# The second MLP product of a diffusion layer as seven block products per pass, with weight sums made by accumulating transfers

## The chip, the core and the metric

The kernel runs on one core of one Trainium2 chip. The metric is device time in microseconds (us), the median of the runs shown. All arithmetic is 32-bit. A large product is made as three TensorE passes: each operand is split into a rounded part ("hi", ScalarE) and the rest ("lo", VectorE), and hi·hi, hi·lo and lo·hi are summed in PSUM. Engines are called as in the profile: PE (TensorE), DVE (VectorE), ACT (ScalarE), POOL (GpSimd) and SP (SyncE, which only issues transfers).

## The reference, cut to what matters

One layer over 512 latent tokens and 256 context tokens of width 1024: modulation vectors from a condition, a modulated norm, an input projection, windowed attention beside a gated delta rule, an output projection with a residual, and an MLP of hidden width 4096 with a second residual. The last step is the one that is changed:

```
def mlp(s, shift, scale_m):
    hm = rms_norm(s, g_norm2) * (1.0 + scale_m) + shift
    return jnp.square(jax.nn.relu(hm @ w_mlp1)) @ w_mlp2
x_new = x_new + gt2 * mlp(x_new, sh2, sc2)
```

## The kernel before, in words

**Front (0 to about 45 us).** SP issues the loads in the order of a list: the latent tokens `xT` (four of 512 KB), the condition, the parameters, then sixteen 512 KB pieces of the modulation weights (`in_wada`, line 148), with three early weight tiles and the context tokens between them. While they land, PE runs 30 matmuls on a tile of ones (line 230, `NONES`); each takes two rows of the trace. `norm_x` squares the tokens on ACT (line 402), adds on DVE (405) and sums over partitions on PE (406); ACT makes the reciprocal root (line 185 is the helper for ACT). For each of eight k-tiles, `ada` multiplies the condition by its weights (249), `columns` turns the row into columns (272) and DVE makes scale and shift (281, 282); `features` modulates (339 on DVE, 340 on ACT, 341 on DVE) and `early_x` feeds the early tiles (331, 333, 335). More ones-matmuls (276 `NWAIT`, 434 `WARM`) stand between these.

**MLP (about 520 us to the end).** The hidden width is worked through in four passes of 1024 (`hf` 0 to 3). Pass 0 makes its part of the first product tile by tile. Passes 1 to 3 make it by class `Pair`: two hidden tiles at a time, as seven block products of half tiles (Strassen's method in Winograd's form; line 1612 issues all its matmuls, 336 of 128x256 in a pass). The operand sums of the weights are made on DVE, in SBUF. `Pair.second` squares the result, splits it and appends it to `act_`.

In each pass the second product follows, channel-major: for each of eight tiles of output channels one load of 512 KB (`w2`, line 290), a split (ACT line 295, DVE line 300), 24 matmuls of 128x512 (8 hidden tiles by 3; lines 331, 333, 335), and one DVE operation (line 1739) that scales the PSUM tile by `gt2` and adds it to the residual `xn_` in SBUF. After pass 3 each `xn_` tile is stored (line 1742), and the host transposes the result.

**Order.** Within an engine the order is set before the run: `Lists` plays the program through with costs and picks the next instruction of each engine by rank; the table `SHIFTS` moves ranks by hand. At run time each engine works through its own list in order and waits on semaphores, so an instruction that waits holds up all that stand behind it on its engine. Buffers of the arena (`alloc`, `free`) come free in program order. POOL issues the transfers that add to their destination (`accum_op`, so far line 298: 16 weight tiles of the input projection get their lo part that way), SP the plain ones.

Of the kernel before, what the change touches and what calls it, by code (L numbers as in the profile page):

```python
# [10 lines left out]
F32 = mybir.dt.float32  # L11
# [18 lines left out]
NONES, NWAIT = 30, 8  # L30
# [8 lines left out]
WARM = (0, 3, 3, 3, 2, 0, 0, 0)  # L39
NROWS = 2  # L40
ND1 = 3
NGD = 5
P = 128
D = 1024
# [73 lines left out]
def tile_layer(ctx: ExitStack, tc: tile.TileContext, I: dict, out: bass.AP, dbg=None):  # L118
# [72 lines left out]

    cc = cload("cc", [P, KT, 2])
# [65 lines left out]
    xs_, cs_ = alloc(8 * SEQ), alloc(8 * CTX)  # L258
    for k2 in range(KT // 2):
        nc.sync.dma_start(out=xs_[:, k2 * 1024:(k2 + 1) * 1024], in_=I["xT"][k2])  # L260
# [86 lines left out]
    for k4 in range(KT // 4):  # L347
        nc.sync.dma_start(out=cs_[:, k4 * 1024:(k4 + 1) * 1024], in_=I["ctxT"][k4])
# [47 lines left out]
    def norm_x():  # L396
        ss = bank()
        for i in range(4):
            b = alloc(1024)
            src = xs_[:, i * 1024:(i + 1) * 1024]  # L400
            n = 512 if i == 3 else 1024
            A.activation(b[:, :n], src[:, :n], AF.Square)
            if i == 3:
                V.tensor_tensor(b[:, n:], src[:, n:], src[:, n:], op=ALU.mult)
            V.tensor_tensor(b[:, :512], b[:, :512], b[:, 512:], op=ALU.add)
            PE.matmul(ss.ap, ones, b[:, :512], start=(i == 0), stop=(i == 3))
            b.free()
        act(rx, ss.ap, AF.Ln, bias=epsc, scale=1.0 / D)
        ss.free()
        return act(rx, rx, AF.Exp, scale=-0.5)  # L410
# [5 lines left out]
    load_early()  # L416
# [5 lines left out]
    features(1)  # L422
    columns(2, ada(2))
    load_early()
# [1142 lines left out]
    class Pair:  # L1567
# [67 lines left out]
        def second(self):  # L1635

            w, z = bank(), bank()
            o = self.o
            self.prod(w[:, :256], "12", "21")
            V.tensor_tensor(o[:, :256], self.u[:, :256], w[:, :256], op=ALU.add)  # L1640
            w.free()
            self.u.free()
            self.prod(z[:, :256], "22", "T4")
            self.prod(z[:, 256:], "S4", "22")
            V.tensor_tensor(o[:, 256:768], o[:, 256:768], z.ap, op=ALU.add)
            z.free()
            A.activation(o.ap, o.ap, AF.Relu)
            A.activation(o.ap, o.ap, AF.Square)
            hi, lo = alloc(1024), alloc(1024)
            split(o.ap, hi.ap, lo.ap)  # L1650
            o.free()
            act_.extend([hi, lo])
            for i in range(2):
                xs.append((r32(hi[:, i * 512:i * 512 + 512]), r32(lo[:, i * 512:i * 512 + 512])))

    def combos():
# [25 lines left out]
        xs7 = {"11": mh[0][:4], "12": mh[0][4:], "22": mh[1][4:]}  # L1682
# [4 lines left out]

    FT = 8
    pairs = [[Pair(hf * FT + f) for f in range(0, FT, 2)] if hf else [] for hf in range(4)]
    for hf in range(4):  # L1690
        act_, xs = [], []
        for f in range(0 if hf else FT):
# [7 lines left out]
            r, hl = alloc(1024), alloc(1024)  # L1700
            A.activation(r[:, :512], acc.ap, AF.Relu)
            acc.free()
            V.tensor_tensor(r[:, 512:], r[:, :512], r[:, :512], op=ALU.mult)
            split(r[:, 512:], hl[:, :512], hl[:, 512:])
            for b in bufs + [r]:
                b.free()
            act_.append(hl)
            xs.append((r32(hl[:, :512]), r32(hl[:, 512:])))
            next(late)
        if hf == 0:  # L1710
            xs7 = combos()
            for _ in late:
                pass
            scr_[0].free()
            for b in MH[0]:
                b.part(1024, 1024).free()
        w2 = lambda ct: wload(I["wm2"][ct * 4 + hf])
# [9 lines left out]
        ws = [w2(0), w2(1)]  # L1727
        if hf:
            ps_[-1].second()
        accs = [bank(), bank()]  # L1730
        ks = list(range(FT))
        for cols in (ks[:FT - 2], ks[FT - 2:]):
            for acc, w in zip(accs, ws):
                mm3(acc.ap, w, [xs[k] for k in cols], start=(cols[0] == 0), stop=(cols[-1] == FT - 1), ks=cols)
        for ct in range(8):
            if ct > 1:
                accs.append(bank())
                mm3(accs[ct].ap, w2(ct), xs)
            V.scalar_tensor_tensor(xn_[ct], accs[ct].ap, modT[:, 3, ct:ct + 1], xn_[ct], op0=ALU.mult, op1=ALU.add)  # L1739
            accs[ct].free()  # L1740
            if hf == 3:
                nc.sync.dma_start(out=out[ct], in_=xn_[ct])
            if hf < 3 and ct in (3, 5):
                (pairs[hf + 1][0].load1 if ct == 3 else pairs[hf + 1][0].load2)()
        for b in act_:
            b.free()
        if hf < 3:
            pairs[hf + 1][1].load1()
# [140 lines left out]
class Lists:  # L1889

    ENGINES = ("PE", "DVE", "Activation", "Pool", "SP")

# [46 lines left out]
    def run(self, rank):  # L1939
# [4 lines left out]
        free, links = [0., 0., 0., 0., 750.], [0., 0., 0., 0., 3200.]  # L1944
# [3 lines left out]
        rows, done = [None, None], [0., 0.]  # L1948
# [22 lines left out]
        for _ in range(n):  # L1971
# [16 lines left out]
            if self.dma[k]:  # L1988
                if e == 4:
                    if len(flight) >= 8:  # L1990
                        t = max(t, flight[-8])
                    links[e] = end = max(t + (2400 if self.bytes[k] > 100000 else 1600), links[e]) + self.bytes[k] / 422
                    flight.append(end)
                    free[e] = t + 400
                else:
                    links[e] = end = max(t + 2400, links[e]) + self.bytes[k] / 159
                    free[e] = t + 900
            else:
                own, lag = self.cost[k]
                if e == 0:  # L2000
                    words, had = words + self.words[k], words
                    block = int(words / 256 + .63)
                    if block > int(had / 256 + .63):
                        asked[block] = max(t + 1100, links[4] - 500) + 1250
                    t = max(t, asked.get(int(had / 256 - .54), 0))
# [5 lines left out]
                if e in (1, 2):  # L2011
                    if self.rows[k] != rows[e - 1]:
                        t, rows[e - 1] = max(t, done[e - 1] + 28), self.rows[k]
                    done[e - 1] = t + lag
                end = t + lag
# [74 lines left out]
def pack(i):  # L2090
# [31 lines left out]
    m2 = i["w_mlp2"][0].reshape(4, 8, P, 8, P)  # L2122
    a["wm2"] = np.ascontiguousarray(m2.transpose(3, 0, 2, 1, 4).reshape(32, P, KT, P))
# [41 lines left out]
```

## Time and profile before, and how to read it

| what | value |
|---|---|
| median of 3 runs | 866.34 us (865.48 to 866.76) |
| the profiled execution | 865.59 us, of which 863.5 us are its span |
| granted TensorE clock, mean | 0.997 |
| PE, DVE, ACT, POOL busy | 98%, 75%, 58%, 3% of the span |
| read from memory, written | 103.61 MB, 2.10 MB |

A busy PE in this table is the union of matmul durations, which overlap: a 128x512 matmul is shown with 0.39 us, while the next one starts 0.23 us later. What a matmul costs is therefore read from the distance of two starts. The same holds, less strongly, for DVE. In the views, a row of the windows gives the stretch, its length, and for each engine the busy time with the number of instructions in brackets; then the granted clock, the mean busy share of the 16 DMA engines, and GB/s. A row of the timeline gives start, duration, engine, line, operation, and tiles with their shapes.

### The profile page before, as it was taken

What the parts mean: (1) busy time and instruction counts of PE and PEld (TensorE: products, weight loads), DVE (VectorE), ACT (ScalarE), POOL (GpSimd) and SP (SyncE); (2) the same over time, 40 slices, a digit from 0 to 9 for tenths busy, and PEclk for the clock granted to TensorE, in tenths of its full rate; (3) what the DMA queues carried; (4) which work ended last, traced back from release to release, by engine and by line L of the source; (5) the groups of instructions that cost most, each with busy time, mean ns of one, the idle gap of its engine ahead of it and who ended that gap; (6) DMA issues with size and microseconds to landing.
All of it is one profiled execution on the core that took longest, in us unless ns stands there. A gap on an engine that the chain in (4) does not pass through costs nothing.

```text
span 863.5 us, 17980 instructions
## 1 busy us (share of the span) xinstructions
PE 849.9 (98%) x7544; PEld 715.2 (83%) x7544; DVE 643.9 (75%) x1113; ACT 497.4 (58%) x882; POOL 26.0 (3%) x42
## 2 busy tenths in 40 slices
PE   9999999999999999899999999999999999999998
PEld 6688778877778777687787899888998899889986
DVE  3865899987779997778758879983875388549541
ACT  5569775487669895577754445651553256326510
POOL 0000011010000002000000000000000000000000
PEclk9999999999999999999999999999999999999999
DMA  9924266542211237633116845733413331343031
GB/s 356 364 75 99 61 149 137 121 98 51 37 38 37 72 93 252 212 124 101 40 52 229 284 139 162 247 119 98 146 50 97 111 135 49 98 145 100 2 121 49
DMA packets 31985, 106.86 MB, mean 124 GB/s; under 512 B 4000, under 2 KB 4512, under 8 KB 31904
## 3 DMA queue, kind: packets, MB, share of 16 engines
q1 hardware_dynamic: 29600, 97.33, 33.8%
q0 software_dynamic: 2304, 8.39, 6.1%
q8 instruction: 59, 0.97, 0.4%
q14 instruction: 22, 0.18, 0.1%
HBM read 103.61 MB, written 2.10 MB: 122 GB/s over the span
## 4 chain that ended last, share of the span: by engine, by line
PE 92%; DVE 3%; ACT 2%; DMA 1%; issue 1%; SPq 0%; ACTq 0%; DVEq 0%
PE banks L331 16%; PE banks L333 16%; PE banks L335 15%; PE banks L1612 14%; PE banks L1148 13%; PE banks L1243 3%; PE banks L1194 2%; PE banks L725 2%; DMA wr<-in_wbr 1%; PE banks L230 1%; PE banks L781 1%; PE banks L714 1%; PE banks L715 1%; PE banks L894 1%; PE banks L566 1%
## 5 line engine op out<-in xcount | busy, mean ns | idle before, releaser
L331 PE MATMUL banks<-m,wh 128*128 128x512 f32 (+1 forms) x568 | 212.2, 375 | 0.5 <-ACT wh L295 0.5
L333 PE MATMUL banks<-m,wh 128*128 128x512 f32 (+1 forms) x568 | 210.6, 371 | 0.0
L335 PE MATMUL banks<-m,wl 128*128 128x512 f32 (+1 forms) x568 | 209.9, 370 | 0.0
L295 ACT ACTIVATE wh<-wr 128x1024 fp32r<-128x1024 f32 (+1 forms) x92 | 90.5, 985 | 143.8 <-PE banks L333 104.5
L331 PEld LDWEIGHTS banks<-m,wh 128*128 128x128 f32 x568 | 107.2, 189 | 18.8 <-ACT wh L295 0.9
L1612 PEld LDWEIGHTS banks<-m,m 128*128 128x128 f32 x1008 | 121.9, 192 | 1.0 <-ACT m L224 0.3
L1612 PE MATMUL banks<-m,m 128*128 128x256 f32 x1008 | 122.6, 283 | 0.0
L335 PEld LDWEIGHTS banks<-m,wl 128*128 128x128 f32 x568 | 106.9, 188 | 18.4 <-issue 0.5
L333 PEld LDWEIGHTS banks<-m,wh 128*128 128x128 f32 x568 | 107.1, 189 | 17.7 <-issue 0.5
L224 ACT ACTIVATE m<-m 128x512 fp32r<-128x512 f32 (+2 forms) x118 | 82.4, 721 | 56.8 <-PE banks L1612 9.0
L1148 PE MATMUL banks<-m,wh 128*128 128x512 f32 x320 | 105.7, 405 | 0.8 <-ACT m L185 0.8
L225 DVE TENSOR_TENSOR m<-m,m 128x512 fp32r<-128x512 f32 (+2 forms) x118 | 91.8, 802 | 17.5 <-ACT m L224 16.8
L300 DVE TENSOR_TENSOR wl<-wr,wh 128x1024 fp32r<-128x1024 f32 (+1 forms) x76 | 84.2, 1108 | 13.3 <-ACT wh L295 10.7
L1739 DVE SCALAR_TENSOR_TENSOR m<-banks,modT,m 128x512 f32<-128x512 f32 x32 | 24.0, 750 | 78.2 <-PE banks L335 78.0
L1148 PEld LDWEIGHTS banks<-m,wh 128*128 128x128 f32 x320 | 59.5, 190 | 13.7 <-ACT m L185 1.0
L1148 PE MATMUL banks<-m,wl 128*128 128x512 f32 x160 | 64.5, 403 | 0.0
L333 PE MATMUL banks<-m,m 128*128 128x256 f32 (+1 forms) x136 | 45.8, 343 | 0.2
L511 DVE SCALAR_TENSOR_TENSOR m<-m,m 128x1024 f32<-128x1024 f32 x32 | 39.0, 1220 | 9.1 <-DMA m<-in_wada 9.0
L331 PE MATMUL banks<-m,m 128*128 128x256 f32 (+1 forms) x136 | 44.8, 340 | 0.2 <-ACT m L340 0.2
L335 PE MATMUL banks<-m,m 128*128 128x512 f32 (+1 forms) x120 | 39.5, 335 | 0.0
L1243 PEld LDWEIGHTS banks<-m,m 64*64 64x64 f32 x1600 | 26.5, 134 | 11.2 <-issue 3.9
L1148 PEld LDWEIGHTS banks<-m,wl 128*128 128x128 f32 x160 | 30.3, 189 | 6.3
(263 smaller groups left out, 1311.7 us busy)
## 6 DMA issues: line engine op xcount, KB each, us to landing
m<-in_wada SPq DMA_DIRECT2D x48, 512.0 KB, 4.8
wr<-in_wm SPq DMA_DIRECT2D x40, 512.0 KB, 3.6
wr<-in_win SPq DMA_DIRECT2D x38, 512.0 KB, 3.7
m<-in_wm SPq DMA_DIRECT2D x24, 512.0 KB, 3.7
wl<-in_win POOLq DMA_DIRECT2D x16, 512.0 KB, 5.6
m<-in_xT SPq DMA_DIRECT2D x8, 512.0 KB, 5.5
wr<-in_wbr SPq DMA_DIRECT2D x16, 256.0 KB, 2.6
wr<-in_wout SPq DMA_DIRECT2D x8, 512.0 KB, 4.5
```

The lines of the kernel that those rows point to most:

```text
L224: A.activation(r32(hi), src, AF.Copy)
L225: (eng or V).tensor_tensor(r32(lo), src, hi, op=ALU.subtract)
L295: upper[0] = A.activation(r32(hi), raw, AF.Copy)
L300: V.tensor_tensor(r32(lo), raw, hi, op=ALU.subtract)
L331: PE.matmul(acc, w[0][:, k, :], xhi, start=(start and i == 0), stop=False)
L333: r = PE.matmul(acc, w[0][:, k, :], xlo, start=False, stop=(end and w[1] is None))
L335: r = PE.matmul(acc, w[1][:, k, :], xhi, start=False, stop=end)
L511: r = V.scalar_tensor_tensor(wa.ap, wa.ap, 0.5, scr_[0].ap, op0=ALU.mult, op1=ALU.mult, accum_out=modT[:, grp, j:j + 1])
L1148: PE.matmul(acc.ap, w[x][:, k, :], hx[k][y], start=(k == p == 0), stop=(k == KT - 1 and p == 2))
L1243: runs[n].append(PE.matmul(out_, w, x, start=True, stop=True).ins.name)
L1612: PE.matmul(dst, r32(self.w[w][i][:, k * P:(k + 1) * P]), xs7[x][k][j], start=(n == 0), stop=(n == 11))
L1739: V.scalar_tensor_tensor(xn_[ct], accs[ct].ap, modT[:, 3, ct:ct + 1], xn_[ct], op0=ALU.mult, op1=ALU.add)
```

## The change

**The second product** becomes seven block products per pass (class `Down`), token-major: tokens are the rows of the PSUM tile, output channels its columns. The activations of a pass (`hb`, unsplit) are halved by hidden index and by token, the weights by hidden index and by output channel. Each product has 24 matmuls of 128x512 (line 1807 to 1809 in the new file), so 168 in a pass. Its left operands are blocks or sums of blocks of `hb`, made and split on DVE and ACT (`left`). Its weight sums are not made on an engine: `pieces` loads four half blocks and lets POOL add further blocks onto them while they are loaded from memory again (line 1733, eight transfers of 512 KB in a pass); 14 half weights are split in each pass. In pass 0 ACT copies the seven PSUM results to SBUF; in passes 1 and 2 ACT copies them and POOL adds them onto those of pass 0 by SBUF-to-SBUF transfers (line 1836, seven of 512 KB in a pass). Before pass 3, `gather` sums them across products by seven more such transfers (line 1874), multiplies by `gt2` laid out as a row, `grow` (made by eight PE transposes, line 1878; DVE, line 1888), and adds the residual from memory (line 1890, eight of 256 KB). The residual got there in pass 0: `park` transposes it on PE (32 transposes of 128x128), copies and stores it. In pass 3 the last sums are made on DVE straight from PSUM (`give`, `end`; lines 1842, 1828, 1865, 1866) and stored.

**The front:** all four `xT` loads come first; the squares are halved between ACT and DVE; the context tokens are loaded later, the second early tile earlier; the ones-matmuls go from 30 to 11, from 8 to 4 and from 11 to 6, with 4 new ones inside `norm_x` (`NSUM`). The costs of `Lists` and the table `SHIFTS` (35 entries before, 68 now) are new.

```diff
-NONES, NWAIT = 30, 8
+NONES, NSUM, NWAIT = 11, 4, 4
-WARM = (0, 3, 3, 3, 2, 0, 0, 0)
+WARM = (0, 2, 2, 2, 0, 0, 0, 0)
+LAHEAD = 1
+GAT = 0, 2
...
-            n = 512 if i == 3 else 1024
-            A.activation(b[:, :n], src[:, :n], AF.Square)
-            if i == 3:
-                V.tensor_tensor(b[:, n:], src[:, n:], src[:, n:], op=ALU.mult)
+            A.activation(b[:, :512], src[:, :512], AF.Square)
+            V.tensor_tensor(b[:, 512:], src[:, 512:], src[:, 512:], op=ALU.mult)
...
-            split(o.ap, hi.ap, lo.ap)
+            A.activation(hb[:, at:at + 1024], o.ap, AF.Square)
...
+        ORDER = ("11", "A11"), ("T3", "S3"), ("T1", "S1"), ("T2", "S2"), ("21", "A12"), ("22", "S4"), ("T4", "A22")
...
+            c = [raw(0, 0, p) for p in two]
+            d = [raw(0, 1, p) for p in two]
+            for p in two:
+                add(d[p], 1, 1, p)
+            for p in two:
+                yield halves(c[p].ap)
+                add(c[p], 0, 1, p)
+            for p in two:
+                yield halves(d[p].ap)
+                add(d[p], 0, 0, p)
+            for p in two:
+                yield halves(c[p].ap)
+                c[p].free()
+            for p in two:
+                yield halves(d[p].ap)
+                add(d[p], 1, 0, p)
+            for k in range(2):
+                for p in two:
+                    yield other(1, k, p)
+            for p in two:
+                yield halves(d[p].ap)
+                d[p].free()
...
+                for p in range(2):
+                    wh, wl = self.ready.pop(0)
+                    for tt in range(2):
+                        zz, ts_ = z[:, tt * 512:tt * 512 + 512], slice(tt * P, tt * P + P)
+                        for k in range(2):
+                            kk = 2 * p + k
+                            PE.matmul(zz, hi[:, kk, ts_], wh[:, k], start=(kk == 0), stop=False)
+                            PE.matmul(zz, hi[:, kk, ts_], wl[:, k], start=False, stop=False)
+                            PE.matmul(zz, lo[:, kk, ts_], wh[:, k], start=False, stop=(kk == 3))
...
+            if self.hf == 0 or self.hf == 3 and w in ("11", "T3", "T1"):
+                accs_[w] = alloc(1024, True)
+                A.activation(accs_[w].ap, z.ap, AF.Copy)
+                return
+            if self.hf < 3:
+                t = alloc(1024)
+                A.activation(t.ap, z.ap, AF.Copy)
+                G.dma_start(out=accs_[w].ap, in_=t.ap, accum_op=ALU.add)
...
+            if w == "T2":
+                e7, t = accs_["T3"], alloc(1024)
+                V.tensor_tensor(t.ap, e1.ap, z.ap, op=ALU.add)
+                add(e7, t)
+                add(t, e5)
+                add(e5, e7)
+                self.end("21", e7)
+                self.end("22", e5, True)
+                accs_["12"] = t
+            elif w == "21":
+                add(e1, z)
+                self.end("11", e1, True)
+            elif w == "22":
+                t = accs_["12"]
+                add(t, z)
+                self.end("12", t, True)
+            else:
+                self.end("21", z, True)
...
+            for tt in range(2):
+                y, t, x = alloc(512), ends[c][:, tt * 512:tt * 512 + 512], src[:, tt * 512:tt * 512 + 512]
+                V.tensor_tensor(y.ap, x, grow[0][:, cols], op=ALU.mult)
+                V.tensor_tensor(t, t, y.ap, op=ALU.add)
+                if store:
+                    nc.sync.dma_start(out=out[2 * r + tt][:, cols], in_=t)
...
-        w2 = lambda ct: wload(I["wm2"][ct * 4 + hf])
...
-                mm3(accs[ct].ap, w2(ct), xs)
-            V.scalar_tensor_tensor(xn_[ct], accs[ct].ap, modT[:, 3, ct:ct + 1], xn_[ct], op0=ALU.mult, op1=ALU.add)
...
+        down.run()
...
-    (0, 1732, 1922, 1869), (-1, 1465, 1789, 55), (-1, 2037, 2118, -523), (-1, 61, 266, -14), (-1, 31, 44, -137),
+    (0, 2862, 3051, 164), (-1, 115, 415, -25), (-1, 7530, 7531, 754), (-1, 4659, 4764, 98), (-1, 2017, 2101, -36),
```

**How rows move: DVE at the end of the program.** Before, the last rows are the splits of weight tiles (`wl`) and the one operation per output tile, which reads its PSUM tile (`banks`):

```order
L300 TENSOR_TENSOR wl_9034<-wr_9031,wh_9033 128x1024
L1739 SCALAR_TENSOR_TENSOR m_5687<-banks,modT,m_5687 128x512
L300 TENSOR_TENSOR wl_9066<-wr_9063,wh_9065 128x1024
L1739 SCALAR_TENSOR_TENSOR m_5687<-banks,modT,m_5687 128x512
L300 TENSOR_TENSOR wl_9098<-wr_9095,wh_9097 128x1024
L1739 SCALAR_TENSOR_TENSOR m_5687<-banks,modT,m_5687 128x512 x3
```

Now the list ends with sums in SBUF (lines 1866) and multiplications by `grow` (`m_8892`, line 1865); the two rows that read `banks` here belong to product T4, the last of all:

```order
L1866 TENSOR_TENSOR m_6697<-m_6697,m_9222 128x512
L1866 TENSOR_TENSOR m_6835<-m_6835,m_9307 128x512
L1865 TENSOR_TENSOR m_9311<-m_9207,m_8892 128x512
L1865 TENSOR_TENSOR m_9343<-banks,m_8892 128x512
L1866 TENSOR_TENSOR m_6835<-m_6835,m_9311 128x512
L1866 TENSOR_TENSOR m_6874<-m_6874,m_9343 128x512
L1865 TENSOR_TENSOR m_9212<-m_9122,m_8892 128x512
L1865 TENSOR_TENSOR m_9339<-banks,m_8892 128x512
L1866 TENSOR_TENSOR m_6874<-m_6874,m_9212 128x512
L1866 TENSOR_TENSOR m_6874<-m_6874,m_9339 128x512
```

Between the first row that reads product T2 (`m_9207<-m_9082,banks`, line 1842) and the end stand 30 DVE rows, ten of 1024 columns and twenty of 512, four of them splits of weights; before, three rows of 512 stand behind the last split.

**POOL in pass 1.** Before, POOL's list ends with fills of zeros that belong to the delta rule, and holds nothing in the MLP:

```order
L298 DMA wl_2618<-in_win 128x1024
L1017 MEMSET m_3508 32x16x32 x4
L1016 MEMSET m_3504 32x16x32 x2
L1409 MEMSET m_3898 32x16x32 x4
L1016 MEMSET m_3504 32x16x32 x2
L1408 MEMSET m_3897 32x16x32 x4
```

Now it goes on with 57 rows of transfers (61 issues). In pass 1 the additions of weights from memory (`in_wm`, to `m_7251` and `m_7253`) and of results (to the seven sums) alternate, each waiting for what it adds:

```order
L1733 DMA m_7253<-in_wm 128x1024
L1836 DMA m_6570<-m_7422 128x1024
L1836 DMA m_6610<-m_7463 128x1024
L1733 DMA m_7251<-in_wm 128x1024
L1836 DMA m_6697<-m_7507 128x1024
L1733 DMA m_7253<-in_wm 128x1024
L1836 DMA m_6739<-m_7550 128x1024
```

So the third addition onto `m_7251` stands behind two additions of results that wait for products 11 and T3.

**SP at the front.** Before, condition and parameters stand between the token loads, and the first weights of the modulation follow:

```order
L260 DMA m_123<-in_xT 128x1024 x2
L148 DMA c_cc<-in_cc 128x16
L148 DMA c_prm<-in_prm 128x188
L260 DMA m_123<-in_xT 128x1024 x2
L148 DMA m_131<-in_wada 128x1024
L148 DMA m_153<-in_wada 128x1024
```

Now the four token loads are first:

```order
L198 DMA m_71<-in_xT 128x1024 x4
L152 DMA c_cc<-in_cc 128x16
L152 DMA c_prm<-in_prm 128x188
L152 DMA m_112<-in_wada 128x1024
L152 DMA m_118<-in_wada 128x1024
L313 DMA wr_124<-in_wab 128x512
```

The last token load moves ahead of two small ones; the first weight pair keeps its place in the sequence.

More of the change, by code (lines that the diff above doesn't have):

```diff
@@ L189, in act @@
         return r
+    xs_, cs_ = alloc(8 * SEQ), alloc(8 * CTX)
+    for k2 in range(KT // 2):
+        nc.sync.dma_start(out=xs_[:, k2 * 1024:(k2 + 1) * 1024], in_=I["xT"][k2])
     cc = cload("cc", [P, KT, 2])
@@ L415, in tile_layer @@
     rp1 = ada(1)
-    load_early()
     norm_x()
@@ L1726, in tile_layer @@
                 ps_[i + 2].load1()
-        ws = [w2(0), w2(1)]
+            if hf == 3 and i in GAT:
+                next(last)
+            if i == 2:
+                down = Down(hf)
+                down.left()
         if hf:
             ps_[-1].second()
[L1730 to L1737, printed above, removed]
-                mm3(accs[ct].ap, w2(ct), xs)
[L1739 to L1746, printed above, removed]
+        if hf == 3:
+            for _ in last:
+                pass
+        down.run()
         if hf < 3:
-            pairs[hf + 1][1].load1()
+            for f in down.loads:
+                f()
     return ties, gangs
```

195 lines of the change are left out of this document (161 added, 34 removed), and 21 rows, old and new, of the table SHIFTS.

## The prediction

> **What bounds the kernel now.** I read the totals first, then the busy time by stretches, then the timeline inside the stretches that change, and last the waits and the transfers.
>
> ```profile
> PE 849.9 (98%) x7544; PEld 715.2 (83%) x7544; DVE 643.9 (75%) x1113; ACT 497.4 (58%) x882; POOL 26.0 (3%) x42
> 691.00:734.00 43.00, 43.00 (x347) 42.22 (x346) 37.05 (x60) 26.43 (x36) 0.00 (x0) 1.00 0.27 91
> 734.00:776.00 42.00, 42.00 (x190) 34.76 (x190) 20.71 (x24) 11.88 (x13) 0.00 (x0) 1.00 0.37 115
> DVE m L1739 <- PE banks L335: 78.0, 24, 4.7
> PE banks L331 <- ACT wh L295: 0.5, 1, 0.5
> ```
>
> The two stretches are pass 2: seven block products for the first MLP product (691 to 734), then the second product (734 to 776). PE is busy throughout both, at clock 1.00. DVE waits 78.0 us for PE at line 1739, while PE's own longest wait for a weight split is 0.5 us. So the MLP is bound by PE, and a PE instruction taken out of it shortens the program as long as nothing else is late. DVE is the next: 57.8 of 85.0 us in this pass.
>
> How long one matmul holds PE is the distance of starts, six apart here:
>
> ```profile
> 819.84 0.39 PE L335 MATMUL banks<-m,wl 128*128 128x512 f32 x1
> 821.20 0.39 PE L335 MATMUL banks<-m,wl 128*128 128x512 f32 x1
> 173.24 0.87 PE banks L725 x8
> ```
>
> (821.20 − 819.84) / 6 = 0.2267 us for a 128x512 matmul. The third row, from the chain that ended last, gives 0.87 / 8 = 0.109 us for a 128x128 transpose.
>
> **The change part by part.**
>
> *Matmuls.* Each pass goes from 8 x 24 = 192 matmuls to 7 x 24 = 168: over four passes 96 x 0.2267 = **21.8 us less**. The residual's transposes (32) and those of the gate row (8) are new on PE: 40 x 0.109 = **4.4 us more**; they stand in PE's list between products, so nothing hides them. A pass now lasts about 85.0 − 5.4 = 79.6 us.
>
> *DVE and ACT in a pass.*
>
> ```profile
> L300 DVE TENSOR_TENSOR wl<-wr,wh 128x1024 fp32r<-128x1024 f32 x60 | 73.2, 1220 | 6.4 <-ACT wh L295 4.1
> L224 ACT ACTIVATE m<-m 128x1024 fp32r<-128x1024 f32 x26 | 27.5, 1056 | 7.3 <-DVE m L1592 4.7 <-DVE m L1589 1.5 <-ACT m L1701 0.9
> L1739 DVE SCALAR_TENSOR_TENSOR m<-banks,modT,m 128x512 f32<-128x512 f32 x32 | 24.0, 750 | 78.2 <-PE banks L335 78.0
> 559.75 1.22 DVE L225 TENSOR_TENSOR m<-m,m 128x1024 fp32r<-128x1024 f32 x1
> 560.88 0.68 DVE L1703 TENSOR_TENSOR m<-m 128x512 f32<-128x512 f32 x1
> 568.80 0.68 DVE L1592 TENSOR_TENSOR m<-m 128x512 f32<-128x512 f32 x1
> 569.41 0.68 DVE L1590 TENSOR_TENSOR m<-m,m 128x512 f32<-128x512 f32 x1
> ```
>
> DVE loses 8 weight splits and 4 activation splits (1.22 us each) and 8 operations of line 1739 (0.75): 20.6 us. It gains 14 weight splits, 7 activation splits and 4 block sums: 25 x 1.22 = 30.5. That makes 57.8 + 9.9 = 67.7 of 79.6 us, 85%. ACT goes from 38.3 by 16 x 1.06 (28 new, 12 gone) to 55.3. Both fit within PE's time in passes 0 to 2, if they fit everywhere within a pass. The tightest place is the end of a pass: behind the last pair 26 DVE rows (20 of 1024, 6 of 512) have to be through before the last half weight is used, some 31 us later. At the spacing of neighbours (1.13 and 0.61, from the starts above) they take 26.3 us, at full durations 28.5. So no wait of PE follows, by a margin of 2.5 to 5 us.
>
> *The end of pass 3.* Here DVE does more: the sums across products and the gate. From the end of product T2 to the end stand 30 DVE rows, ten of 1024 and twenty of 512 columns: 10 x 1.13 + 20 x 0.61 = 23.5 us when none waits for its neighbour, 25.9 when all do; few do, and I take 23.7. PE has three products left, 72 x 0.2267 = 16.3 us. DVE is busy up to that point (14 rows of 1024 in the two products before), so it can't begin early, and it works in order. It ends 23.7 + 0.1 − 16.3 = 7.5 us behind PE. Before, the last matmul starts at 859.28 and lasts 0.39, and one operation of 0.75 follows:
>
> ```profile
> 859.28 0.39 PE L335 MATMUL banks<-m,wl 128*128 128x512 f32 x1
> 859.71 0.75 DVE L1739 SCALAR_TENSOR_TENSOR m<-banks,modT,m 128x512 f32<-128x512 f32 x1 [4.69 <-PE banks L335]
> ```
>
> That is 0.8 us, so the end costs **6.7 us more** (between 6.5 and 8.9). The store after it stays 256 KB.
>
> *Transfers.*
>
> ```profile
> q1 hardware_dynamic: 29600, 97.33, 33.8%
> q0 software_dynamic: 2304, 8.39, 6.1%
> wl<-in_win POOLq DMA_DIRECT2D x16, 512.0 KB, 5.6
> L298 POOL DMA_DIRECT2D wl<-in_win x16: 862/865/1007, 69.8 to 252.4; - x16
> ```
>
> The sixteen adding transfers of before cost POOL 0.87 us each, land after 5.6 us, and keep the 16 DMA engines busy for 0.061 x 863.5 / 16 = 3.29 us each. A plain one of the same 512 KB takes 0.338 x 863.5 x 0.524 / 97.33 = 1.57 us. A pass has 16 plain ones before and after; new in passes 1 and 2 are 15 adding ones: 25.1 + 49.4 = 74.5 of 79.6 us. The Trainium skill says, in "DMA: Bandwidth & Descriptors", section "Issuing engines are not separate DMA queues", that transfers from all engines run on the same 16 DMA engines and interleave; by it there is no second road for POOL's additions, which speaks against this change. From the rows: the first additions are issued in the first half of a pass. The third addition onto a half block is issued about 14 us into the second product, behind two additions of results; two or three times 3.29 us later it has landed, before 26 us, and is needed at 30. So I count nothing certain for it. For waits in all (transfers, changeovers, ACT's order) the trace gives 0 to 5.6 us, one exposed landing; I take **1.5 us more**, nearer the 0.5 us above, once for each of three changeovers.
>
> *Front.*
>
> ```profile
> 1.34 9.00 PE L230 MATMUL banks<-ones 128*128 128x128 f32 x60 [1.34 <-DVE onec L201]
> 10.18 1.88 PE L406 MATMUL banks<-m,ones 128*128 128x512 f32 x4
> 14.58 0.69 ACT L185 ACTIVATE m<-banks,epsc 128x512 f32<-128x512 f32 x1 [3.60 <-PE banks L406]
> 17.68 0.74 DVE L339 SCALAR_TENSOR_TENSOR m<-m,modA,m 128x512 f32<-128x512 f32 x1
> 2.00:10.00 8.00, 8.00 (x58) 8.00 (x58) 1.65 (x6) 4.52 (x6) 0.00 (x0) 1.00 0.97 351
> 20.00:30.00 10.00, 8.94 (x81) 5.49 (x79) 8.75 (x20) 5.54 (x12) 0.00 (x0) 1.00 1.03 420
> 30.00:40.00 10.00, 9.90 (x84) 6.94 (x76) 9.36 (x21) 5.80 (x12) 1.47 (x2) 1.00 0.88 333
> 5.00:6.00 1.00, 1.00 (x8) 1.00 (x8) 1.00 0.95 234
> 6.00:7.00 1.00, 1.00 (x11) 1.00 (x11) 1.00 1.02 352
> ```
>
> The sum of squares stands behind 60 rows of ones until 10.18, and the root starts at 14.58. With 22 rows PE is free near 5 us. Four token tiles (2.1 MB at 351 GB/s, 6 us) have landed by about 8.3; square, add and matmul follow in 2.4, so the root can start near 10.8, 3.8 us earlier, and so can the first modulation (17.68). From 20 to 40 us DVE is 91% busy and can't catch up or lose much, so the lead is kept unless the loads, which fill the DMA engines to 30 us, hold it up (gain 0). I take **3.0 us less**. On the other side, ones-matmuls come at 8 rows per us before 6 us and at 11 after, both at clock 1.00: should the shorter warm-up leave PE slow, the eight rows of line 406 (3.9 us) would take 3.9 x 11 / 8 = 5.4, a loss of 1.5. "TensorE: Matmul & The Clock Gate" of the Trainium skill, section "Why this matters for your kernels", asks for about 4 us of unbroken matmuls and no gaps over about 3 us; by it the slow start would last, and the sum would be 1.5 us higher. The fences show one speed change, near 6 us, with no gap before it.
>
> *Sum.* −21.8 + 4.4 + 6.7 + 1.5 − 3.0 = −12.2 us. The profiled execution took 865.59 us (span 863.5), the median is 866.34: 853.4 on the first, **854 us** on the second.
>
> **The rivals.**
>
> *The end is hidden.* DVE gets through the last sums beside PE, for instance because the splits of the last products run well ahead. Then the 6.7 us fall away: 847 us. For it: ACT and POOL are idle there. Against it: DVE's list is fixed, and T2 is needed by all the sums.
>
> *DVE is late at the changeovers too.* 85% busy leaves 12 us per pass; if half weights come one landing (5.6 us) later than needed, less the smaller margin of 2.5, each of the three changeovers loses 3 us: 854 + 9 = 863 us. For it: full durations and a late transfer together use up the margin.
>
> *Slower: the DMA engines are the bound.* In the second half of passes 1 and 2, 12 adding and 8 plain transfers need 12 x 3.29 + 8 x 1.57 = 52.0 us, PE 38.1. Two result sums (6.6) can slip into the next pass; 7.3 us remain, twice. Pass 3 holds 15 adding ones, 16 plain ones and eight halves from memory (13.2): 87.7 against 79.6, 8.1 over. If all that lands on weights, 22.7 us: 877 us. It decides where a third addition lands later than 30 us after product 11 starts. For it: POOL's list is in order, and weights stand behind results. Against it: results are not urgent, and the plain loads are issued early.
>
> *No net change.* Waits at their upper bound, a slow front and a long end (−21.8 + 4.4 + 8.9 + 5.6 + 1.5 = −1.4) come close to 866.
>
> **How the numbers follow.** My forecast has a chance of 0.55, the hidden end 0.12, late changeovers 0.17, the DMA bound 0.12, no net change 0.04. The first three are faster: 0.84; slower 0.12. About 0.2%, 1.7 us, is what a measurement here can tell from no change. The range takes in the first three: from 846, just under the hidden end, to 865, where the upper bounds of waits, front and end add up.
>
> **What would show it.** In the new profile: 168 matmuls of lines 1807 to 1809 in each second product at 0.227 us; DVE rows of lines 1865 and 1866 running about 7.5 us past the last matmul, without waiting for PE; PE's waits in the MLP short; the root near 11 us and first modulation near 14. Wrong would be: PE idle for weight splits whose releaser is an adding transfer, above all in the third additions; a DMA share near 1 in the second halves; or an end under 2 us.

## The result and the profile after

The changed kernel took 890.26 us (median of 4 runs, 888.38 to 892.35), the kernel before 866.55 us beside it (865.48 to 868.6): 1.0271 times as long, with a 95% interval of 1.0239 to 1.0304. It is 24 us slower where 12 us less were forecast. The profiled execution took 892.35 us (span 890.6).

From the page of the changed kernel: busy times, the queue that GpSimd issues on, and the engines' shares of the chain that ended last.

```profile
PE 845.8 (95%) x7440; PEld 701.7 (79%) x7440; DVE 706.7 (79%) x1162; ACT 557.7 (63%) x946; POOL 79.4 (9%) x103
q0 software_dynamic: 11088, 38.28, 24.2%
PE 61%; DMA 15%; DVE 11%; issue 6%; ACT 5%; POOL 1%; SPq 0%; ACTq 0%; DVEq 0%; POOLq 0%
```

PE executes 104 rows fewer, yet it is no longer busy throughout (95% of the span, 98% before), and 15% of the chain is transfers. The queue that GpSimd issues on went from 6.1% to 24.2% of 16 engines.

The MLP by passes: each stretch runs from the first matmul of a second product (line 1807) to that of the next pass, the last one to the last matmul. Columns: length, busy time of PE, PEld, DVE, ACT, POOL, granted clock, DMA share, GB/s.

```profile
559.56:645.56 86.00, 82.34 (x502) 72.97 (x500) 67.00 (x89) 58.25 (x74) 4.72 (x6) 0.96 0.51 148
645.56:737.83 92.27, 86.85 (x542) 77.06 (x541) 68.33 (x90) 55.13 (x68) 13.46 (x16) 0.98 0.80 187
737.83:835.87 98.04, 83.98 (x490) 74.37 (x489) 67.25 (x88) 53.68 (x66) 22.58 (x26) 0.91 0.95 214
835.87:879.00 43.13, 41.08 (x193) 34.02 (x192) 41.62 (x44) 22.87 (x24) 7.94 (x9) 1.00 0.67 134
```

A pass should have taken 79.6 us and takes 86 to 98. PE stands idle for 3.7 + 5.4 + 14.1 + 2.1 = 25.2 us, and the clock below 1 takes at most 0.04 x 86.0 + 0.02 x 92.3 + 0.09 x 98.0 = 14.1 us (less, since some of the low clock falls into the stops: from 768 to 770 us it is 0.60 and PE does nothing). The DMA share is highest, 0.95 over a whole pass, where the loss is largest.

What PE waited for, and then what the waited-for engines had waited for (from the waits of PE, ACT and DVE: us in total, times, longest).

```profile
PE banks L1807 <- ACT wh L231: 12.0, 5, 4.5
PE banks L1619 <- ACT m L231: 7.7, 3, 6.4
...
ACT m L231 <- DMA m<-in_wm: 24.2, 10, 5.1
ACT wh L231 <- DMA m<-in_wm: 16.3, 6, 6.3
...
ACT wh L231 <- DMA wr<-in_wm: 5.8, 4, 1.9
...
DVE m L1596 <- DMA m<-in_wm: 20.2, 5, 5.3
```

Before, the profile shows no wait of PE in the MLP; the 0.5 us for a weight split that the prediction quotes lie ahead of it. Now PE waits 12.0 us for splits of the second product's weights and 7.7 us for those of the next pairs (line 1619). Behind both stand transfers, and not only adding ones: `wr<-in_wm` and the loads that line 1596 reads are plain. One such place, in pass 1 (the matmuls of line 1807 up to it, the SP queue, ACT, PE):

```profile
L1807 PE MATMUL banks<-wh,m x40: 387/389/402, 645.6 to 677.1; 128*128 128x512 f32 x40
...
671.02 16.03 SPq L1742 DMA_DIRECT2D wr<-in_wm  x4
...
680.38 1.06 ACT L231 ACTIVATE wh<-wr 128x1024 fp32r<-128x1024 f32 x1 [1.95 <-DMA wr<-in_wm]
...
681.48 0.73 PE L1807 MATMUL banks<-wh,m 128*128 128x512 f32 x2 [3.57 <-ACT wh L231]
```

Forty matmuls of line 1807 are five products: PE stops ahead of the sixth, whose half blocks are plain loads into the ring of two raw buffers. The two other long stops are at the same product of pass 2 and at the third pair of pass 3:

```profile
770.40 1.22 PE L1807 MATMUL banks<-wh,m 128*128 128x512 f32 x2 [4.54 <-ACT wh L231]
805.92 0.79 PE L1619 MATMUL banks<-m,m 128*128 128x256 f32 x2 [6.42 <-ACT m L231]
```

The end (last matmul, last row of DVE), then the front: the root, then the modulation (line 343, 339 before) and the residual rows (line 1497, 1490 before), each with its first and last start, after and before.

```profile
879.07 0.39 PE L1809 MATMUL banks<-wh,m 128*128 128x512 f32 x1
885.46 1.40 DVE L1866 TENSOR_TENSOR m<-m,m 128x512 f32<-128x512 f32 x2
```

```profile
11.89 0.69 ACT L189 ACTIVATE m<-banks,epsc 128x512 f32<-128x512 f32 x1 [0.78 <-PE banks L407]
L343 DVE SCALAR_TENSOR_TENSOR m<-m,modA,m x16: 474/610/746, 15.1 to 43.9; 128x512 f32<-128x512 f32 x8, 128x256 f32<-128x256 f32 x8
L1497 DVE SCALAR_TENSOR_TENSOR m<-banks,gt1h,m x11: 477/485/751, 475.2 to 516.6; 128x256 f32<-128x256 f32 x6, 128x512 f32<-128x512 f32 x5
```

```profile
L339 DVE SCALAR_TENSOR_TENSOR m<-m,modA,m x16: 473/608/746, 17.7 to 43.6; 128x512 f32<-128x512 f32 x8, 128x256 f32<-128x256 f32 x8
L1490 DVE SCALAR_TENSOR_TENSOR m<-banks,gt1h,m x11: 476/487/751, 479.9 to 521.0; 128x256 f32<-128x256 f32 x6, 128x512 f32<-128x512 f32 x5
```

DVE ends 886.86 − 879.46 = 7.4 us behind PE. The first modulation is 2.6 us earlier than before, the last 0.3 us later; the first residual row is 4.7 us earlier.

### The profile page after: what moved, and what is told of

The parts are those of the page before. It is cut to its first block, busy times and chain, and to the rows that moved or that the text cites. A ratio compares the mean times of both kernels' runs of the same rounds, so it can differ in the third digit from the quotient of the medians.

```text
span 890.6 us, 18148 instructions
## 1 busy us (share of the span) xinstructions
PE 845.8 (95%) x7440; PEld 701.7 (79%) x7440; DVE 706.7 (79%) x1162; ACT 557.7 (63%) x946; POOL 79.4 (9%) x103
## 3 DMA queue, kind: packets, MB, share of 16 engines
q0 software_dynamic: 11088, 38.28, 24.2%
## 4 chain that ended last, share of the span: by engine, by line
PE 61%; DMA 15%; DVE 11%; issue 6%; ACT 5%; POOL 1%; SPq 0%; ACTq 0%; DVEq 0%; POOLq 0%
PE banks L1155 13%; DMA m<-in_wm 7%; PE banks L335 7%; PE banks L337 7%; PE banks L339 6%; PE banks L1619 5%; PE banks L1250 3%; DVE m L232 3%; PE banks L1201 3%; PE banks L1808 2%; PE banks L1809 2%; PE banks L1807 2%; DMA m<-in_wada 2%; DMA m<-m 2%; PE banks L732 2%
## 5 line engine op out<-in xcount | busy, mean ns | idle before, releaser
L231 ACT ACTIVATE m<-m 128x512 fp32r<-128x512 f32 (+2 forms) x126 | 94.8, 769 | 85.5 <-DMA m<-in_wm 24.2
L335 PE MATMUL banks<-m,wh 128*128 128x512 f32 (+1 forms) x312 | 112.4, 362 | 0.2 <-ACT wh L299 0.2
L337 PE MATMUL banks<-m,wh 128*128 128x512 f32 (+1 forms) x312 | 110.7, 357 | 0.0
L339 PE MATMUL banks<-m,wl 128*128 128x512 f32 (+1 forms) x312 | 110.2, 356 | 0.5 <-DVE wl L304 0.5
L1807 PE MATMUL banks<-wh,m 128*128 128x512 f32 x224 | 88.9, 404 | 12.0 <-ACT wh L231 12.0
L1808 PE MATMUL banks<-wl,m 128*128 128x512 f32 x224 | 90.5, 404 | 2.3 <-DVE wl L232 2.3
L1809 PE MATMUL banks<-wh,m 128*128 128x512 f32 x224 | 89.5, 404 | 0.2 <-DVE m L232 0.2
L1155 PEld LDWEIGHTS banks<-m,wh 128*128 128x128 f32 x320 | 58.7, 188 | 14.8 <-ACT m L189 1.9
L339 PEld LDWEIGHTS banks<-m,wl 128*128 128x128 f32 x312 | 58.8, 189 | 9.8 <-DVE wl L304 1.2
L335 PEld LDWEIGHTS banks<-m,wh 128*128 128x128 f32 x312 | 59.0, 189 | 9.3 <-ACT wh L299 1.1
L337 PEld LDWEIGHTS banks<-m,wh 128*128 128x128 f32 x312 | 59.0, 189 | 8.3 <-issue 0.7
L1807 PEld LDWEIGHTS banks<-wh,m 128*128 128x128 f32 x224 | 43.4, 195 | 22.9 <-ACT wh L231 14.1
L231 ACT ACTIVATE wh<-m 128x1024 fp32r<-128x1024 f32 x40 | 41.9, 1054 | 24.5 <-DMA m<-in_wm 16.3
L304 DVE TENSOR_TENSOR wl<-wr,wh 128x1024 fp32r<-128x1024 f32 (+1 forms) x44 | 45.1, 1024 | 14.5 <-ACT wh L299 14.3
L1808 PEld LDWEIGHTS banks<-wl,m 128*128 128x128 f32 x224 | 43.6, 195 | 12.9 <-DVE wl L232 3.8
```

The costliest lines, as they stand in the source:

```text
L231: A.activation(r32(hi), src, AF.Copy)
L304: V.tensor_tensor(r32(lo), raw, hi, op=ALU.subtract)
L335: PE.matmul(acc, w[0][:, k, :], xhi, start=(start and i == 0), stop=False)
L337: r = PE.matmul(acc, w[0][:, k, :], xlo, start=False, stop=(end and w[1] is None))
L339: r = PE.matmul(acc, w[1][:, k, :], xhi, start=False, stop=end)
L1155: PE.matmul(acc.ap, w[x][:, k, :], hx[k][y], start=(k == p == 0), stop=(k == KT - 1 and p == 2))
```

## The experiments

Theory A: the adding transfers take so much of the 16 DMA engines that everything that moves in the MLP lands late, plain loads too. The rivals were B (the new order on the engines), C (too much work on VectorE and ScalarE at the ends of passes) and D (weights queued behind results in GpSimd's list). All runs but e8, e10 and e12 keep the changed kernel's order row by row; e6 puts 52 rows into it, and in e11 the copy and the adding transfer of a result become one row of DVE. e1 to e5 and e9 leave sums out: they price the loss and are no kernels to use.

**e1: all adding transfers plain.** The three other lines (1836, 1874, 1890) likewise:

```
-                G.dma_start(out=t.ap, in_=src[k, n, p], accum_op=ALU.add)
+                G.dma_start(out=t.ap, in_=src[k, n, p])
```

> The instruction order of the changed kernel on every engine, but all 61 adding transfers of the second MLP product (weight sums, result sums, sums at the end) are plain copies of the same bytes from the same queue; the sums themselves are left out. Theory A (the adding transfers fill the 16 DMA engines, so everything that moves in the second products lands late): the waits of TensorE and the lower clock go, 846 to 858 us. Theory B (the new order and its list places are what costs): 885 to 892, as the order is kept. Theory C (VectorE and ScalarE have too much work at the ends of the passes): 885 to 892, as their work is kept. Theory D (weights stand behind results in GpSimd's list, which waits for ScalarE's copies): 880 to 890, as the list is kept and only the landing gets shorter.

Measured 867.74 us, ratio to before 1.0013 (0.9995 to 1.0031). 22.5 us of the loss go with the same bytes, the same queue, the same order and the same waits: B, C and D can't be the main cause. But it isn't the 846 to 858 that A gave. The queue's row of this page:

```profile
q0 software_dynamic: 10576, 38.28, 15.9%
```

In the changed kernel 0.242 x 890.6 / 73 = 2.95 us of 16 engines per adding transfer (38.28 MB are 73 times 512 KB). Here 16 in the middle of the kernel still add; the other 57 take (0.159 x 866.5 − 16 x 2.95) / 57 = 1.59 us each. Adding costs 1.36 us more than copying, 57 times: 77.5 us of DMA time.

**e2 and e3: a part of them plain**, e2 only the weight sums (line 1733), e3 only the result sums.

> As the changed kernel in order, but the 32 weight sums alone are plain transfers (the sums of the weights are left out; the result sums still add). Theory A: 32 of 61 lose about half of their DMA time, roughly half of what all plain ones win back, 862 to 875 us. Theories B and C: 885 to 892. Theory D: 882 to 890.

> As the changed kernel in order, but the result sums (lines 1836, 1874, 1890) are plain copies, the weight sums still add (the sums of results are left out). Theory A: the other half, 862 to 875 us; if the weight sums' own landing is what counts rather than the shared engines, 880 to 890. Theories B and C: 885 to 892. Theory D: 882 to 890.

Measured 879.85 us (1.0159, 1.0130 to 1.0188) and 875.43 us (1.0114, 1.0073 to 1.0155): 10.4 and 14.8 us won, together 25.2, about what e1 wins (22.5). Both kinds of sum bear a share. e3 lies just above its 875; e2 is 5 us above its range.

**e4, e9 and e5: next to no bytes**, in e4 the result sums, in e9 the weight sums, in e5 both:

```
-                G.dma_start(out=accs_[w].ap, in_=t.ap, accum_op=ALU.add)
+                G.dma_start(out=accs_[w][:, :16], in_=t[:, :16], accum_op=ALU.add)
```

> As the changed kernel in order, but each result sum (lines 1836, 1874, 1890) moves and adds only 16 of its columns (most of the sums of results is left out); the weight sums still add in full, and every wait in GpSimd's list is kept. Theory A: nearly all of the result sums' DMA time goes, more than in the run with plain ones, 852 to 868 us. Theories B and C: 885 to 892. Theory D, GpSimd's list with its waits: as in the run with plain result sums, within 3 us, and above 880.

> As the changed kernel in order, but the 32 weight sums alone move and add only 16 of their columns (most of the sums of weights is left out); the result sums add in full. Theory A, one shared stock of DMA time: 32 of the 57 full-size adding transfers go, so somewhat more is won than with tiny result sums (20 us), or at least as much: 862 to 870 us. If only what stands ahead of the loads of the weights counts (the result sums), less: 872 to 880.

> As the changed kernel in order and in all waits, but all 61 adding transfers of the second MLP product move and add only 16 of their columns (most of the sums of weights and results is left out). Theory A in its strict form (only what the adding transfers take of the 16 DMA engines costs): all waits of TensorE in the second products go, and what is left is the forecast without its waits, 848 to 856 us. If the plain copies of the run before were no burden any more, and the rest is VectorE's and ScalarE's (theory C for the remainder): 864 to 869, as with plain copies.

Measured 870.17 us (e4: 1.0054, 1.0035 to 1.0074), 869.27 us (e9: 1.0057, 1.0034 to 1.0081) and 853.53 us (e5: 0.9857, 0.9832 to 0.9882). e9 is in the range of theory A; e4 is 2 us above its own, but 5 below e3, which copies the same results in full: GpSimd's list and its waits are all there, so theory D falls, and bytes are what costs. e5 by passes, its queue, and the one wait of PE for a split in it:

```profile
558.79:636.75 77.96, 77.96 (x501) 71.03 (x500) 61.17 (x83) 56.34 (x72) 4.38 (x6) 1.00 0.43 136
636.75:720.45 83.70, 83.70 (x542) 75.89 (x541) 68.86 (x91) 55.41 (x68) 13.94 (x17) 1.00 0.37 103
720.45:798.58 78.13, 76.99 (x490) 69.89 (x489) 66.39 (x87) 53.09 (x66) 22.53 (x26) 1.00 0.42 111
798.58:839.40 40.82, 40.82 (x193) 34.07 (x192) 40.66 (x43) 22.85 (x24) 7.93 (x9) 1.00 0.18 41
...
q0 software_dynamic: 11088, 8.89, 7.9%
...
PE banks L1619 <- DVE m L232: 0.9, 1, 0.9
```

But for that 0.9 us and less, PE is busy throughout at clock 1.00, with DVE's and ACT's work unchanged (DVE 40.66 of 40.82 us in the last stretch): theory C falls too. Against the changed kernel the four stretches are 8.0, 8.6, 19.9 and 2.3 us shorter, 38.8 together, which is the difference of the spans (38.9). So the whole loss lies in the MLP, half of it in pass 2 and the first products of pass 3, and goes with the bytes of the adding transfers. As plain copies they cost 14.2 us (e1 less e5), as additions 22.5 more. e9 and e4 tell which sums cost where (the first and the third stretch of e9, then of e4):

```profile
558.09:636.06 77.97, 77.97 (x501) 71.04 (x500) 61.41 (x84) 56.46 (x73) 4.97 (x7) 1.00 0.41 136
722.07:813.97 91.90, 80.97 (x490) 71.86 (x489) 66.25 (x87) 52.71 (x65) 22.21 (x26) 0.96 0.73 178
...
558.53:643.05 84.52, 80.02 (x502) 70.64 (x501) 65.54 (x88) 58.25 (x74) 4.81 (x6) 1.00 0.50 148
731.64:812.73 81.09, 77.69 (x491) 69.75 (x490) 66.63 (x87) 53.15 (x66) 22.36 (x26) 1.00 0.69 164
```

Without the weight sums' bytes (e9) pass 0 is as short as in e5, and the third stretch still takes 91.9 us; without the result sums' (e4) it is the other way about. The loss of pass 0 is that of the weight sums, and most of the loss of the third stretch that of the result sums.

**e6: idle time filled.** 14, 14 and 24 matmuls of ones ahead of the three long stops quoted above:

```
+                    if (self.hf, n, p) in ((1, 5, 0), (2, 5, 0)):
+                        fill(z[:, :P], 14)
...
+            if self.f == 28 and w == "T2":
+                fill(dst[:, :P], 24)
```

> The changed kernel with its transfers, and 52 matmuls of ones (128 columns) put into TensorE's list at the three places where it stood idle longest (3.6, 4.5 and 6.4 us); they need nothing that is late. Theory: the granted clock falls because TensorE stood idle, and that is 10 us or more of the loss: with the gaps filled the clock stays near 1 and the time falls to 876 to 884 us, though nothing lands earlier. Rival: the clock falls for another reason, or what it costs would have been waited for anyway as the transfers are late by as much: 887 to 894.

Measured 891.6 us (1.0292, 1.0271 to 1.0313): the rival was right. Pass 2 of this run, then a stop in pass 0 of the changed kernel and the clock beside it:

```profile
738.01:834.80 96.79, 89.24 (x567) 80.11 (x566) 66.92 (x88) 53.50 (x66) 22.55 (x26) 0.98 0.95 218
...
568.97 0.51 PE L1807 MATMUL banks<-wh,m 128*128 128x512 f32 x1 [1.09 <-ACT wh L231]
570.00:575.00 5.00, 4.48 (x13) 3.59 (x14) 4.19 (x5) 5.00 (x7) 0.86 (x1) 0.66 0.51 79
```

In pass 2 the clock goes from 0.91 to 0.98, which is worth 0.07 x 97 = 6.8 us of PE, and the pass is 1.3 us shorter. What the low clock takes would else have been spent waiting: the transfers set the pace there. "TensorE: Matmul & The Clock Gate" of the Trainium skill, section "Why this matters for your kernels", asks for no gaps over about 3 us; the stops of 4.5 and 6.4 us and the clock of 0.91 agree with it, but here filling them gained nothing. The trace goes further than this rule: in pass 0, where no stop is longer than 1.1 us, the clock fell too (0.66 in the row above).

**e7: result sums on GpSimd.** Lines 1836 and 1874 as additions, nothing left out:

```
-                G.dma_start(out=accs_[w].ap, in_=t.ap, accum_op=ALU.add)
+                G.tensor_tensor(accs_[w].ap, accs_[w].ap, t.ap, op=ALU.add)
```

> As the changed kernel in order, but the 21 result sums of lines 1836 and 1874 are additions on GpSimd instead of adding transfers; nothing is left out. Theory A: as with tiny result sums (870 us), or up to 5 us more if GpSimd's additions last over 2 us and hold up the weight sums behind them: 868 to 876. If GpSimd slows VectorE beside it, or holds up the weights by more than the adding transfers did: 880 and up.

Measured 896.25 us (1.0353, 1.0328 to 1.0377), in the range of the second case. Rows of POOL and DVE beside each other (two additions, one DVE operation), and the third stretch of the MLP:

```profile
788.20 5.66 POOL L1874 TENSOR_TENSOR m<-m,m 128x1024 f32<-128x1024 f32 x2
...
791.52 2.89 DVE L1596 TENSOR_TENSOR m<-m,m 128x512 f32<-128x512 f32 x1
...
738.94:839.84 100.90, 84.20 (x491) 73.19 (x490) 94.95 (x87) 53.14 (x66) 50.21 (x26) 0.95 0.55 136
```

An addition takes GpSimd 2.8 us (5.66 for two), and a DVE operation of 512 columns beside it 2.89 us where the same line takes 0.69 in a run without such additions (e10, below). VectorE, which the splits need, is busy for 94.95 us in the third stretch (last row) where it was 67.25: the relief of the DMA engines is lost to it. "SBUF — State Buffer" of the Trainium skill, section "SBUF: two separate sides", says that for operations like these (two inputs in SBUF on VectorE, and GpSimd reading SBUF) one of the two holds a shared port pair for its whole instruction while the other fully blocks; the 2.89 us, as long as the addition itself, agree.

**e8: the front alone.** The new front, planner and list places ahead of the MLP, with the MLP of before (the list places are cut at the first instruction of the second products):

> The front, the planner and the list places of the changed kernel for everything ahead of the MLP, and the MLP of the kernel before. Theory (the front's lead is gone by the first weight product, and 4 to 5 us are won between 250 and 480 us): 860 to 863 us. By the prediction's own term for the front (3.0 us): 863. If the list places only pay together with the new MLP: 866 or more.

Measured 868.51 us (1.0028, 1.0015 to 1.0041): neither 863 nor less, but the last case. Its first residual rows, and a stop that neither kernel has:

```profile
L1497 DVE SCALAR_TENSOR_TENSOR m<-banks,gt1h,m x11: 475/486/751, 473.9 to 521.7; 128x256 f32<-128x256 f32 x6, 128x512 f32<-128x512 f32 x5
...
527.56 1.01 PE L335 MATMUL banks<-m,m 128*128 128x256 f32 x3 [3.59 <-ACT m L344]
```

The lead ahead of the MLP is there (the first residual row at 473.9 against 479.9) and is gone by the last one (521.7 against 521.0); the stop of 3.59 us follows. That it goes because the two sets of list places meet there is not shown. What the front and the middle are worth by themselves stays open.

**e10, e11 and e12: two ways to lighten it that keep the result.** e10 loads the two last plain half blocks of passes 1 and 2 into buffers that come free earlier. e11 adds the results of passes 1 and 2 on VectorE. e12 does both.

```
                 yield halves(c[p].ap)
-                c[p].free()
+                nc.sync.dma_start(out=c[p].ap, in_=src[1, 1, p])
...
-                A.activation(t.ap, z.ap, AF.Copy)
-                G.dma_start(out=accs_[w].ap, in_=t.ap, accum_op=ALU.add)
+                V.tensor_tensor(accs_[w].ap, accs_[w].ap, z.ap, op=ALU.add)
```

> The changed kernel, but in passes 1 and 2 the two last plain half blocks of each pass are loaded into the buffers of the first two, which come free some two products earlier than the ring of two raw buffers; the sums are the same and nothing is left out. Theory A, backlog: the transfers are as many and as long, so earlier issue moves the wait to another transfer: 882 to 890 us. Rival: the waits come from loads that are issued too late because the ring is short: the two longest waits on them (3.6 and 4.5 us) and what follows them go, 872 to 881.

> The changed kernel's order, but the 14 result sums of passes 1 and 2 are additions on VectorE straight from PSUM in place of ScalarE's copy and an adding transfer; nothing is left out. Theory A: passes 1 and 2 gain as with tiny result sums, pass 3 keeps its seven sums: 872 to 878 us, if VectorE has room (67.7 and 8.5 of 79.6 us). Theory C (VectorE too full): 880 and up.

> Both edits together, the earlier loads and the result sums of passes 1 and 2 on VectorE, in an order that the planner makes; nothing is left out. Theory A: with 22 adding transfers fewer at work in the second products the earlier loads can use the free time, 866 to 876 us; it beats the kernel before only if the weight sums are then hidden (below 865).

Measured 907.86 us (e10: 1.0482, 1.0461 to 1.0503), 878.18 us (e11: 1.0138, 1.0119 to 1.0157) and 895.8 us (e12: 1.0337, 1.0315 to 1.0360). e11 is at the upper end that theory A gave; e12 misses its range by 20 us with the edit of e10 in it. e10 went against both theories. Its pass 1, SP, DVE and PE:

```profile
659.44 3.13 SPq L1759 DMA_DIRECT2D m<-in_wm  x2
...
678.82 0.69 DVE L1599 TENSOR_TENSOR m<-m 128x512 f32<-128x512 f32 x1 [4.74 <-DMA m<-in_wm]
...
684.72 0.69 DVE L1596 TENSOR_TENSOR m<-m,m 128x512 f32<-128x512 f32 x1 [4.08 <-DMA m<-in_wm]
...
687.19 1.22 DVE L232 TENSOR_TENSOR wl<-m,wh 128x1024 fp32r<-128x1024 f32 x1
...
688.47 0.80 PE L1816 MATMUL banks<-wl,m 128*128 128x512 f32 x1 [4.76 <-DVE wl L232]
```

The earlier loads (line 1759) go ahead of the next pair's load, which now is the late one. DVE's list is in order, stands 4.7 and 4.1 us for it, and the weight split that PE waits for (687.19) is behind it. So what gets a head start pushes another back, as A says; that the sum is 18 us worse was not foreseen, and since the planner also made another order of this kernel, the run does not part the two. No version here that keeps all sums beats the kernel before.

## Why the prediction was wrong, step by step

- **Matmuls**: right. The four stretches of e5, nearly without waits, add up to 280.6 us; four second products of 168 x 0.2267 us and three first products of 43.0 (the prediction's first stretch) make 281.4.
- **The end**: right; 7.5 us forecast, 7.4 measured (8.2 in e5).
- **Front**: the size is near, the place is not. 3.0 us less were forecast because the root starts earlier; it does (11.89 for 14.58, forecast 10.8, as PE is free of the ones at 6.1 us and not near 5), but the last modulation is no earlier (43.9 for 43.6), the lower bound of 0 that the step named. 4.7 us were won after that, up to the residual, which no step forecast; one part is a stop of PE of 2.59 us in the kernel before, ahead of 347.37, that is gone.
- **VectorE and ScalarE fit**: right; in e5 PE's wait for them is 0.9 us, quoted above.
- **Waits, "0 to 5.6 us, one exposed landing; I take 1.5 us more"**: this is the step that failed. By e5 the bytes of the adding transfers cost 36.7 us (890.26 − 853.53). The other terms held together: they give 852.5 us without this one, and e5 took 853.53. That they meet so closely is in part luck, as the lead at the residual was 4.7 us instead of 3.0.

The step failed in its argument, not in its price. A price of 3.29 us per adding transfer was too high if anything (2.95), and 74.5 of 79.6 us per pass was worked out. It then asked only whether the *third addition* lands in time, and counted "nothing certain for it". The runs show three things in its place. First, what the three long stops wait for are plain loads: the half blocks of the sixth product and the loads of the next pairs, which the step counted in its budget but not among what could land late. Their landing gets later with the adding transfers (plain half blocks, line 1742, and pair loads, line 1592, first in the changed kernel and then in e5):

```profile
DMA to landing us min/median/max: 3.3/6.9/13.1
...
DMA to landing us min/median/max: 3.5/5.0/10.9
...
DMA to landing us min/median/max: 3.4/4.0/6.2
...
DMA to landing us min/median/max: 3.4/3.6/4.6
...
662.22 11.12 SPq L1742 DMA_DIRECT2D wr<-in_wm  x4
```

Late issue is not the reason for the stop in pass 1: the first of its half blocks is issued 25.5 us after the start of the second product in both kernels (671.02 − 645.56, and 662.22 − 636.75 in e5, last row). It lands some 9 us later in the changed kernel (the split at 680.38 waits for it), and soon enough in e5 that PE does not stop.

Second, such a budget is no fit: 25.1 + 15 x 2.95 = 69.4 of 79.6 us, 87% (94% by the forecast's price). The loads on SP's queue wait until splits on DVE free their buffers (first row below), so the DMA engines don't always have work ahead: their share is 0.98 in one stretch of pass 1 and 0.42 in the next but one (the second number from the right):

```profile
SPq L1592 <- DVE m L232: 126.3, 12, 23.8
...
650.00:675.00 25.00, 25.00 (x126) 20.76 (x126) 20.61 (x20) 20.04 (x22) 6.82 (x8) 1.00 0.98 201
700.00:725.00 25.00, 23.68 (x191) 22.87 (x190) 18.47 (x31) 12.67 (x18) 0.00 (x0) 1.00 0.42 117
```

Third, pass 0 and the first products of pass 3 lose as well. Pass 0 has no result sums, and its 8.0 us go with its eight weight sums (77.97 us in e9, above), which the budget left out since it looked at passes 1 and 2. In pass 3 the last result sums and the seven sums across products are issued on GpSimd's queue within 30 us, from the first to the last of ten:

```profile
775.42 0.86 POOL L1836 DMA_DIRECT2D m<-m  x1 [12.79 <-ACT m L1835]
...
804.62 0.88 POOL L1874 DMA_DIRECT2D m<-m  x1 [0.24 <-issue]
```

That is 10 x 2.95 = 29.5 us of all 16 engines, and the load that PE waits for until 805.92 has to share them.

**The rival that came true** was "the DMA engines are the bound": 877 us, with 22.7 us for the waits, at a chance of 0.12. Its mechanism is in the main the one that the runs show, but for the loads that came late: it had weight additions behind result sums in mind, and held against itself that "the plain loads are issued early". Its size was too small: it left out pass 0 (8.0 us), and had 22.7 us where the other three stretches lost 30.8. It compared sums of busy time (52.0 against 38.1 us). That it also took a transfer's delay for the delay of PE, where an engine that works in order and stands for one late load holds up the splits behind it, is argued and not measured (e10 shows such rows). "DMA: Bandwidth & Descriptors" of the Trainium skill, section "Issuing engines are not separate DMA queues", which the prediction cites against the change (all issuers share the same 16 DMA engines), was borne out: loads on SP's queue got late through additions on GpSimd's.

Of the signs named beforehand, PE idle for weight splits and a DMA share near 1 in the second halves both came, but the transfers behind the three long stops are plain. The third additions were not where it showed: in pass 1 the first of them was issued 20 us into the second product instead of 14 (at 665.61), and yet PE did not stop for the seventh product, which needs them.

## What to carry to other kernels

A transfer that adds cost 2.95 us of all 16 DMA engines where a copy of the same bytes cost 1.59, so moving additions from a busy engine to the transfers has to be paid from the DMA budget of the very stretch, with the plain loads in it; here a budget of 0.87 of the pass was already too much, since loads could not run ahead of their buffers. Ask of each engine that works in order not only whether its work fits, but which late transfer it would stand for, and what is behind that. To price such a change before building it fully, shrink the transfers to a few columns and keep the order: e5 showed in one run that all other terms of the sum held together within about 1 us.

## What was unexpected of the hardware

An addition on GpSimd slowed the operations of VectorE beside it from 0.69 to 2.89 us, so idle time of GpSimd was no free time. And the low granted clock of pass 2 cost nothing of its own: with the stops filled it rose from 0.91 to 0.98, 6.8 us of PE, and the kernel took 891.6 us instead of 890.3.
